# Two feed-forward half steps of a hybrid decoder layer: block products of 2x2 Strassen form in place of plain tiled products

## The chip, the cores and the metric

One core of a Trainium2 chip runs the whole step. The metric is device time in microseconds (us) of one launch. All arithmetic is float32: every large product is made from operands that are split in two float32r parts (a rounded "hi" and the rest "lo"), as hi·hi + hi·lo + lo·hi, so one product of a 128x128 weight tile and 260 tokens is three matmuls.

## The reference

One layer on 520 tokens (512 of a prompt and 8 single sample tokens), width 1024, feed-forward width 2816, followed by a final RMSNorm:

```python
x = x + 0.5 * swiglu(rmsnorm(x, n1), wg1, wu1, wd1)      # half step 1
x = x + token_mix(rmsnorm(x, nm), ...)                   # SSD scan heads and short conv, w_in, w_out
x = x + 0.5 * swiglu(rmsnorm(x, n2), wg2, wu2, wd2)      # half step 2
y = rmsnorm(x, nf)
def swiglu(x, wg, wu, wd): return (silu(x @ wg) * (x @ wu)) @ wd
```

## The kernel before

Activations lie with channels on the 128 partitions and the 520 tokens along the free axis, in two halves of 260 tokens; a matmul takes one weight tile (128x128) and one half.

A **weight unit** is up to eight such tiles of one output tile, 512 KB. `Core.fetch` and `split_w` (L89 to L92) load it on SP's queue into one of two `st` buffers, ScalarE rounds it to `hi` (L91), VectorE subtracts it to `lo` (L92); three pairs of buffers hold units that are ready, and the list `order` in `build` gives their sequence. `mm_unit` and `mm_k` (L115 to L124) walk the tiles of a unit with three products and two halves each, into a PSUM tile of two banks.

`ffn` (L270 and after) runs each half step. For each of 22 hidden tiles it makes the gate product and the up product (8 k-tiles each, 96 matmuls together), then on VectorE and ScalarE the factor of the norm, SiLU, the product of both and the two parts `hh`, `hl` (L283 to L291). For each of 8 output tiles it makes the way down over the 22 hidden tiles (132 matmuls), adds it to `x` (L299) and calls `after`, which prepares what the next stage needs: `Next` scales and splits x (L178, L179) and sums its squares on GpSimd (`square`, L143 to L147). Between the half steps stands `mixer` (L356 on). The last output tile of half step 2 is made by token halves, so that the final norm of the first half (`last`, L322 to L350) runs while the second is multiplied.

Instructions are put on the engines' queues by a scheduler that goes by its own timeline; each engine takes its queue in order. In the half steps GpSimd has nothing to do except the squares behind an output tile.

```python
 91  self.S.copy(hi, st)                                            # per weight unit, ScalarE
 92  self.V.tensor_tensor(lo, st, hi.bitcast(F32), op=ALU.subtract) # per weight unit, VectorE
```

Of the kernel before, what the change touches and what calls it, by code (L numbers as in the profile page):

```python
# [62 lines left out]

class Core:
    """The pieces that every phase uses: weight units, products, norm factors."""

    def __init__(self, nc, tc, ctx, a, order):
# [26 lines left out]
    def fetch(self):  # L94
        if self.at == len(self.order):
            return
        src, nk, *dt = self.order[self.at]
        self.at += 1
        st = self.wst.tile([P, KU, P], F32, tag="st", name="st")
        hi, lo = self.parts()  # L100
        if any(dt):  # both parts of the few dt weights in one stationary operand
            self.nc.sync.dma_start(st, src)
            s = slice(2 * NH, 3 * NH)
            self.S.copy(hi, st)
            self.V.tensor_tensor(hi[:, :, s], st[:, :, s], hi[:, :, s].bitcast(F32), op=ALU.subtract)
        else:
            self.split_w(src, st[:, :nk], hi[:, :nk], lo[:, :nk])
        self.ready.append((hi, lo, nk))

    def unit(self, ahead=1):  # L110
        while len(self.ready) < 1 + ahead and self.at < len(self.order):
            self.fetch()
        return self.ready.pop(0)

    def mm_k(self, ps, hi, lo, k, xh, xl, first, last, hs=(0, 1)):  # L115
        for n, (w, x) in enumerate(((hi, xh), (hi, xl), (lo, xh))):
            for h in hs:
# [18 lines left out]
    # RMSNorm: squares summed over the channel tiles here, over the partitions by a  # L136
    # product with ones; the factor of each token goes in behind the next product
# [3 lines left out]
    def square(self, acc, xt, first, eng):  # L141
        if first:
            eng.tensor_tensor(acc, xt, xt, op=ALU.mult)  # L143
        else:
            sq = self.nrm.tile([P, T], F32, tag="sq", name="sq", bufs=1)
            eng.tensor_tensor(sq, xt, xt, op=ALU.mult)  # L146
            eng.tensor_tensor(acc, acc, sq, op=ALU.add)  # L147

    def factor(self, accs, width):
        with self.tc.high_priority(2000):  # L150
            return self._factor(accs, width)

    def _factor(self, accs, width):
        r = self.nrm.tile([P, T], F32, tag="r", name="r")
        if len(accs) == 1:  # in two parts that sum to it
            ones = self.onesr
            hi = self.nrm.tile([P, T], F32R, tag="ah", name="ah", bufs=1)
            lo = self.nrm.tile([P, T], F32R, tag="al", name="al", bufs=1)
            self.S.copy(hi, accs[0])
            self.V.tensor_tensor(lo, accs[0], hi.bitcast(F32), op=ALU.subtract)  # L160
            accs = [hi, lo]
        else:
            ones = self.ones
        for h in range(2):
            hs = slice(h * H2, (h + 1) * H2)
            ps = self.bank()
            for i, acc in enumerate(accs):
                self.PE.matmul(ps[:, :H2], ones, acc[:, hs], start=i == 0, stop=i == len(accs) - 1)  # L168
            self.S.activation(r[:, hs], ps[:, :H2], AF.Sqrt, bias=self.eps, scale=1.0 / width)
            self.V.reciprocal(r[:, hs], r[:, hs])  # L170
        return r

    # what a product needs of x: x times the norm weight in two float32r parts
    def x_parts(self):
        return [self.xp.tile([P, KD, T], F32R, tag=n, name=n) for n in ("xh", "xl")]

    def split_x(self, xt, xh, xl, w):
        self.S.activation(xh, xt, AF.Copy, scale=w)  # L178
        self.V.scalar_tensor_tensor(xl, xt, w, xh.bitcast(F32), op0=ALU.mult, op1=ALU.subtract)  # L179
# [27 lines left out]

def build(nc, tc, ctx, a, o):
    order = []
    for f in range(1, KF):  # L210
        order += [(a["wg1"][f], KD), (a["wu1"][f], KD)]
    down = lambda w: [(w[d][:, k:min(k + KU, KF)], min(KU, KF - k)) for d in range(KD) for k in range(0, KF, KU)]
    order += down(a["wd1"])
    order += [(a["wi"][i], KD, i == 0) for i in range(a["wi"].shape[0])]
    for d in range(0, KD, 2):
        order += [(a["wo"][e][:, h:h + KD], KD) for h in (KD, 0) for e in (d, d + 1)]
    for f in range(KF):
        order += [(a["wg2"][f], KD), (a["wu2"][f], KD)]
    order += down(a["wd2"])
    c = Core(nc, tc, ctx, a, order)  # L220
# [4 lines left out]
    c.onesr = c.cst.tile([P, P], F32R, name="onesr")  # L225
    V.tensor_copy(c.onesr, c.ones)
# [4 lines left out]
    # the tensor engine's clock comes up while the first loads are under way  # L231
# [4 lines left out]
    # ---- input, with the first two weight units cut in pieces so that the products  # L236
    # can follow the loads
    x = [c.xp.tile([P, T], F32, tag=f"x{k}", name=f"x{k}") for k in range(KD)]
    xh, xl = c.x_parts()
    acc = [c.new_acc(), c.new_acc()]  # L240
    c0 = ExitStack()
    tp = c0.enter_context(tc.tile_pool(name="t0", bufs=2))
    u0 = [(a[w][0], tp.tile([P, KU, P], F32, tag="st", name="st")) + c.parts() for w in ("wg1", "wu1")]
    ps0 = [c.psum(), c.psum()]
    nc.sync.dma_start(c.pc, a["pc"])
    for k in range(KD):
        for h in range(2 if k == 0 else 1):
# [540 lines left out]
```

## Time and profile before

| | |
|---|---|
| median of 3 runs | 1196.25 us (1195.64 to 1198.01) |
| the profiled execution | span 1193.0 us from first to last instruction; its time outside the span is not given, the median is 3.25 us above the span |
| TensorE busy | 1163.1 us, 97% of the span, 9583 matmuls |
| VectorE, ScalarE, GpSimd busy | 632.9 (53%), 384.1 (32%), 254.0 us (21%) |
| granted TensorE clock, mean | 0.993 |
| half step 1, mixer, half step 2 | to about 395 us, to about 807 us, to the end |

A busy share is an average over stages with different limits, so a stage is read by itself. Spans of neighbouring instructions of one engine overlap by some tens of ns; where a price matters, the distance from one start to the next is taken.

### The profile page before, as it was taken

To read this page: it belongs to the slowest core of one execution; us is meant where nothing else is said; L and a number is where in the kernel's file an instruction comes from. 1 tells how busy PE (TensorE), PEld (TensorE's weight loads), DVE (VectorE), ACT (ScalarE), POOL (GpSimd) and SP (SyncE) were. 2 spreads that over 40 slices of the span, in tenths; PEclk is the share of its full clock that TensorE was granted. 3 is DMA by queue.
4 is the path that set the end of the run, shared out by engine and by line. 5 is a ranking of instruction groups with operands and counts; after the bars stand their busy time and mean duration, and the time that the engine had idled before them with its cause. 6 is when DMAs were issued, how large, how long until landed. Compare 5 with 4: busy or idle time off the path is not lost.

```text
span 1193.0 us, 22147 instructions
## 1 busy us (share of the span) xinstructions
PE 1163.1 (97%) x9583; PEld 1150.2 (96%) x9583; DVE 632.9 (53%) x810; ACT 384.1 (32%) x524; POOL 254.0 (21%) x318
## 2 busy tenths in 40 slices
PE   8999999999999999998899999999999999999996
PEld 7999999999999999987889999999999999999996
DVE  7544444443333678889987476445444444432224
ACT  5322222222222466344332343223222222222221
POOL 4000000000222377567643232320000000001112
PEclk8999999999999999999999999999999999999998
DMA  5322222222332432455533222222222222232322
GB/s 197 101 96 89 89 89 92 101 87 80 98 95 89 123 107 95 144 186 166 187 107 95 78 89 91 103 90 90 89 89 92 100 93 89 90 97 81 98 81 72
DMA packets 50361, 122.99 MB, mean 103 GB/s; under 512 B 9880, under 2 KB 19256, under 8 KB 50264
## 3 DMA queue, kind: packets, MB, share of 16 engines
q1 hardware_dynamic: 50264, 121.58, 31.4%
q8 instruction: 75, 1.23, 0.4%
q14 instruction: 22, 0.18, 0.0%
HBM read 114.43 MB, written 7.14 MB: 102 GB/s over the span
## 4 chain that ended last, share of the span: by engine, by line
PE 87%; POOL 4%; DVE 4%; issue 2%; DMA 2%; ACT 1%; SPq 0%; DVEq 0%; POOLq 0%; ACTq 0%
PE mmt L118 85%; POOL st L623 1%; POOL up L622 1%; DMA out_ss<-st 1%; DMA x<-in_xT 1%; DVE lo L92 1%; DMA st<-in_ssm 1%; DVE s L561 0%; POOL t L654 0%; POOL t L653 0%; DVE s L541 0%; PE auxt L168 0%; PE mmt L403 0%; POOL xd L616 0%; DVE up L625 0%
## 5 line engine op out<-in xcount | busy, mean ns | idle before, releaser
L118 PE MATMUL mmt<-xh,hi 128*128 128x260 f32 x2112 | 429.3, 284 | 1.7 <-ACT xh L178 1.7
L118 PE MATMUL mmt<-xh,lo 128*128 128x260 f32 x2112 | 426.8, 284 | 1.0 <-DVE lo L92 1.0
L118 PE MATMUL mmt<-xl,hi 128*128 128x260 f32 x2112 | 426.8, 284 | 0.8 <-DVE xl L179 0.7
L91 ACT CAST hi<-st 128x1024 fp32r<-128x1024 f32 (+2 forms) x202 | 202.6, 1005 | 644.0 <-issue 361.7
L92 DVE TENSOR_TENSOR lo<-st,hi 128x1024 fp32r<-128x1024 f32 (+2 forms) x202 | 245.2, 1215 | 177.9 <-ACT hi L91 176.7
L118 PEld LDWEIGHTS mmt<-xh,hi 128*128 128x128 f32 x2112 | 327.1, 189 | 2.8 <-ACT xh L178 1.9
L118 PEld LDWEIGHTS mmt<-xh,lo 128*128 128x128 f32 x2112 | 326.6, 189 | 1.8 <-DVE lo L92 1.6
L118 PEld LDWEIGHTS mmt<-xl,hi 128*128 128x128 f32 x2112 | 325.8, 189 | 1.6 <-DVE xl L179 1.5
L118 PE MATMUL mmt<-hh,hi 128*128 128x260 f32 x704 | 146.5, 285 | 0.0
L118 PE MATMUL mmt<-hh,lo 128*128 128x260 f32 x704 | 145.7, 283 | 0.0
L118 PE MATMUL mmt<-hl,hi 128*128 128x260 f32 x704 | 144.5, 281 | 0.0
L143 POOL TENSOR_TENSOR acc<-x 128x520 f32<-128x520 f32 x4 | 5.4, 1349 | 560.2 <-DVE x L299 538.0
L118 PEld LDWEIGHTS mmt<-hl,hi 128*128 128x128 f32 x704 | 110.6, 189 | 0.0
L118 PEld LDWEIGHTS mmt<-hh,hi 128*128 128x128 f32 x704 | 110.5, 189 | 0.1
L118 PEld LDWEIGHTS mmt<-hh,lo 128*128 128x128 f32 x704 | 109.3, 188 | 0.0
L287 DVE TENSOR_TENSOR h<-mmt,g 128x520 f32<-128x520 f32 x44 | 30.8, 700 | 124.3 <-PE mmt L118 124.2
L283 DVE TENSOR_TENSOR g<-mmt,r 128x520 f32<-128x520 f32 x44 | 30.8, 699 | 122.9 <-PE mmt L118 122.9
L146 POOL TENSOR_TENSOR sq<-x 128x520 f32<-128x520 f32 x22 | 35.4, 1609 | 196.6 <-DVE x L299 129.8
L147 POOL TENSOR_TENSOR acc<-acc,sq 128x520 f32<-128x520 f32 x28 | 43.8, 1563 | 2.2
L179 DVE SCALAR_TENSOR_TENSOR xl<-x,pc,xh 128x520 fp32r<-128x520 f32 (+1 forms) x25 | 32.8, 1323 | 4.8 <-ACT xh L178 4.8
L285 DVE TENSOR_TENSOR g<-g,r 128x520 f32<-128x520 f32 x44 | 30.4, 694 | 1.4 <-ACT g L284 1.4
L291 DVE TENSOR_TENSOR hl<-h,hh 128x520 fp32r<-128x520 f32 x44 | 30.5, 694 | 0.7 <-ACT hh L290 0.7
(193 smaller groups left out, 1015.2 us busy)
## 6 DMA issues: line engine op xcount, KB each, us to landing
st<-in_wi SPq DMA_DIRECT2D x45, 512.0 KB, 3.5
st<-in_wg SPq DMA_DIRECT2D x43, 512.0 KB, 3.5
st<-in_wu SPq DMA_DIRECT2D x43, 512.0 KB, 3.4
st<-in_wd SPq DMA_DIRECT2D x32, 512.0 KB, 3.4
st<-in_wo SPq DMA_DIRECT2D x16, 512.0 KB, 3.6
st<-in_wd SPq DMA_DIRECT2D x16, 384.0 KB, 3.1
st<-in_ssm SPq DMA_DIRECT2D x16, 256.0 KB, 2.8
s<-scr SPq DMA_DIRECT2D x8, 512.0 KB, 4.7
```

What stands on the lines that cost most here:

```text
L91: self.S.copy(hi, st)
L92: self.V.tensor_tensor(lo, st, hi.bitcast(F32), op=ALU.subtract)
L118: self.PE.matmul(ps[:, h, :H2], w[:, k, :], x[:, h * H2:(h + 1) * H2], start=first and n == 0, stop=last and n == 2)
L146: eng.tensor_tensor(sq, xt, xt, op=ALU.mult)
L147: eng.tensor_tensor(acc, acc, sq, op=ALU.add)
L179: self.V.scalar_tensor_tensor(xl, xt, w, xh.bitcast(F32), op0=ALU.mult, op1=ALU.subtract)
L283: V.tensor_tensor(halves(g), pg[:, :, :H2], halves(r), op=ALU.mult)
L285: V.tensor_tensor(g, g, r, op=ALU.mult)
L287: V.tensor_tensor(halves(hf), pu[:, :, :H2], halves(g), op=ALU.mult)
L291: V.tensor_tensor(b_, hf, a_.bitcast(F32), op=ALU.subtract)
L622: G.tensor_tensor(up, bb, xd.unsqueeze(2).broadcast_to([P, HB, NS]), op=ALU.mult)
L623: G.tensor_tensor(st, st, up, op=ALU.add)
```

## The change

Both operands of each feed-forward product are cut 2x2: the weights in output tiles m = 0, 1 and k-tiles in pairs, the activations in pairs of k-tiles and the two token halves. Seven block products of the Strassen-Winograd form replace eight.

- **Items.** A load (`load`) now brings a pair of output tiles and n pairs of k-tiles, four blocks a11, a12, a21, a22 of n·128 columns, 2048 columns (1 MB) for a gate or up item. `adds` makes four sums of blocks, S, in one buffer (pool `sp`, one buffer): s2 = a21 + a22, s0 = s2 - a11, s1 = a11 - a21, s3 = a12 - s0, all on GpSimd, except that s1 goes to VectorE where n is 3 or less. `split` then rounds and subtracts as before, but seven blocks instead of four: three units of two blocks (a11 and a12; s0 and s1; s2 and s3) and one of a22.
- **Groups.** `group` runs the seven block products of an item (`block`, 3n matmuls each) into three PSUM banks X, Z, Y of which X goes on accumulating while ScalarE copies its states out (`keep`) and VectorE adds bank and copy (`put`). There are 11 pairs of a gate and an up group (n = 4, 84 matmuls a group) in each half step.
- **Hidden tiles.** `variants` makes the seven operand blocks of a pair (three plain, four sums on VectorE) and their two parts. The product with the norm factor after SiLU (L407) goes to GpSimd.
- **Way down** in four chunks of hidden pairs (`CH`: 3, 3, 3, 2 pairs), of which three stand between a gate and an up group; in each chunk four groups add into `x`: VectorE adds the bank (L440), GpSimd adds ScalarE's copies (L442, three per group).
- **Around it.** `Blocks` scales x and makes its operand blocks at the start of a half step, `Plain` does what `Next` did for the mixer, squares behind a tile go to ScalarE. The final norm has both token halves of the last pair of tiles behind the last group. The mixer's products are as before; its buffers share memory with the new operands, and the scratch for S exists only inside a half step.

```diff
-    def split_w(self, src, st, hi, lo):
-        self.nc.sync.dma_start(st, src)
-        self.S.copy(hi, st)
-        self.V.tensor_tensor(lo, st, hi.bitcast(F32), op=ALU.subtract)
...
+    def adds(self):
+        for item in self.loaded:
+            kind, r, n, s = item[:4]
+            if kind != "S" or self.sp is None:
+                return
+            if s is None:
+                s = self.sp.tile([P, 4, 512], F32, tag="S", name="S")[:, :, :n * P]
+                item[3] = s
+                a11, a12, a21, a22 = (r[:, b] for b in range(4))
+                G = self.G
+                G.tensor_tensor(s[:, 2], a21, a22, op=ALU.add)
+                G.tensor_tensor(s[:, 0], s[:, 2], a11, op=ALU.subtract)
+                e = G if n > 3 else self.V
+                e.tensor_tensor(s[:, 1], a11, a21, op=ALU.subtract)
+                G.tensor_tensor(s[:, 3], a12, s[:, 0], op=ALU.subtract)
+                return
...
+            src = (r[:, :2], s[:, :2], s[:, 2:], r[:, 3])[step]
+            item.append(True)
+            hi, lo = self.parts(src, src.shape[1:])
+            self.both(src, hi, lo)
...
+    def block(self, ps, w, v, n, B, first, last):
+        hi, lo = (t.rearrange("p (k m) -> p k m", m=P) for t in w)
+        for k in range(n):
+            xh, xl = B(v, k)
+            for i, (a, b) in enumerate(((hi, xh), (hi, xl), (lo, xh))):
+                self.PE.matmul(ps[:, :H2], a[:, k, :], b, start=first and k + i == 0, stop=k == n - 1 and i == 2,
+                               skip_group_check=True)
...
+        w = self.take()
+        self.block(X, of2(w, 0), 0, n, B, True, True)
+        ev.p1(X)
+        self.block(Z, of2(w, 1), 1, n, B, True, True)
+        ev.c11(Z)
+        self.split()
+        w = self.take()
+        self.block(X, of2(w, 0), 5, n, B, False, True)
+        ev.u2(X)
+        self.block(Y, of2(w, 1), 4, n, B, True, True)
+        self.split()
+        w, w4 = self.take(), self.take()
+        self.block(X, of2(w, 0), 3, n, B, False, True)
+        ev.u4(X)
+        ev.c22(Y)
+        self.block(Y, w4, 6, n, B, False, True)
+        ev.c21(Y)
+        self.split()
+        self.block(X, of2(w, 1), 2, n, B, False, True)
+        ev.c12(X)
...
+    def c12(self, X):
+        c, g, r = self.c, self.dst, self.r
+        c.V.tensor_tensor(g[:, 0, T1], X[:, :H2], r[:, T1], op=ALU.mult)
+        c.V.tensor_tensor(g[:, 0, T0], g[:, 0, T0], r[:, T0], op=ALU.mult)
+        c.V.tensor_tensor(g[:, 1], g[:, 1], r, op=ALU.mult)
+        c.S.activation(g, g, AF.Silu)
+        c.G.tensor_tensor(g, g, r.unsqueeze(1).broadcast_to([P, 2, T]), op=ALU.mult)
```

The queues show it best in half step 1. First VectorE, in the gate and up stage. Before, one hidden tile has six rows (`g`, `h` its gate and up values, `st` a loaded weight unit, `hi` and `lo` its parts):

```order
L283 TENSOR_TENSOR g_1032<-mmt_922,r_293 128x520
L92 TENSOR_TENSOR lo_1046<-st_1044,hi_1045 128x1024
L285 TENSOR_TENSOR g_1032<-g_1032,r_293 128x520
L287 TENSOR_TENSOR h_1036<-mmt_923,g_1032 128x520
L92 TENSOR_TENSOR lo_1100<-st_1098,hi_1099 128x1024
L291 TENSOR_TENSOR hl6_1039<-h_1036,hh6_1038 128x520
```

Now the piece from one split of S to the same split of the next item (about half of what a pair of groups has; `pst` is a bank, `cp` ScalarE's copy, `raw` a loaded item, `S` its sums, `t4` the sums of a hidden pair):

```order
L149 TENSOR_TENSOR lo_2046<-S_1935,hi_2045 128x1024
L403 TENSOR_TENSOR g_1952<-pst_1953,r_233 128x260
L263 TENSOR_TENSOR hl_1941<-t4_1942,hh_1940 128x1040
L149 TENSOR_TENSOR lo_2067<-raw_1810,hi_2066 128x512
L382 TENSOR_TENSOR g_1952<-pst_1955,cp_1999 128x260
L405 TENSOR_TENSOR g_1952<-g_1952,r_233 128x520
L149 TENSOR_TENSOR lo_2109<-raw_1933,hi_2108 128x1024
L149 TENSOR_TENSOR lo_2139<-S_2072,hi_2138 128x1024
L382 TENSOR_TENSOR h_2077<-pst_2080,cp_2154 128x260
L420 TENSOR_TENSOR h_2077<-h_2077,g_1952 128x260
L149 TENSOR_TENSOR lo_2171<-S_2072,hi_2170 128x1024
```

The rows that read a bank are short; the rest take both operands from SBUF, and the split of S_2072 now waits on another engine's work.

That engine is GpSimd. Before, between the first norm's squares and the first output tile of the way down, it had no row at all; its neighbouring rows are these:

```order
L147 TENSOR_TENSOR acc_106<-acc_106,sq_226 128x520
L143 TENSOR_TENSOR acc_305<-x0_96 128x520
```

Now the same stretch of GpSimd that belongs to the VectorE rows above, a pair of groups:

```order
L132 TENSOR_TENSOR S_1935<-raw_1810 128x512
L135 TENSOR_TENSOR S_1935<-raw_1810 128x512
L133 TENSOR_TENSOR S_1935<-S_1935,raw_1810 128x512
L136 TENSOR_TENSOR S_1935<-raw_1810,S_1935 128x512
L132 TENSOR_TENSOR S_2072<-raw_1933 128x512
L135 TENSOR_TENSOR S_2072<-raw_1933 128x512
L133 TENSOR_TENSOR S_2072<-S_2072,raw_1933 128x512
L136 TENSOR_TENSOR S_2072<-raw_1933,S_2072 128x512
L407 TENSOR_TENSOR g_1952<-g_1952,r_233 128x1040
```

Eight sums of weight blocks and one long product per pair of groups stand where nothing stood.

## Rows read from the trace of the kernel before

**Rows 1.** Head and part 1 of the page: span, busy time of each engine.
```profile
span 1193.0 us, 22147 instructions
PE 1163.1 (97%) x9583; PEld 1150.2 (96%) x9583; DVE 632.9 (53%) x810; ACT 384.1 (32%) x524; POOL 254.0 (21%) x318
```
**Rows 2.** Stretches of half steps: PE, PEld, DVE, ACT, POOL busy, clock, DMA share, GB/s.
```profile
26.73:395.21 368.48, 368.48 (x3070) 368.48 (x3070) 152.79 (x170) 100.04 (x123) 21.46 (x13) 1.00 0.29 94
806.98:1172.00 365.02, 365.02 (x3042) 365.02 (x3041) 142.89 (x162) 98.39 (x122) 19.43 (x13) 1.00 0.28 89
```
**Rows 3.** Timeline of DVE at 396 us: start, length, instruction, shapes.
```profile
396.08 0.70 DVE L146 TENSOR_TENSOR sq<-x 128x520 f32<-128x520 f32 x1
396.69 1.22 DVE L92 TENSOR_TENSOR lo<-st,hi 128x1024 fp32r<-128x1024 f32 x1
397.83 0.17 DVE L446 TENSOR_SCALAR nega<-nega 128x16 f32<-128x16 f32 x1
```
**Rows 4.** Timeline at 777 us, DVE and POOL.
```profile
777.11 2.09 DVE L92 TENSOR_TENSOR lo<-st,hi 128x1024 fp32r<-128x1024 f32 x1 [0.19 <-ACT hi L91]
779.12 1.80 DVE L179 SCALAR_TENSOR_TENSOR xl<-x,pc,xh 128x520 fp32r<-128x520 f32 x1
777.07 1.05 POOL L146 TENSOR_TENSOR sq<-x 128x520 f32<-128x520 f32 x1 [1.89 <-DVE x L716]
778.20 2.17 POOL L147 TENSOR_TENSOR acc<-acc,sq 128x520 f32<-128x520 f32 x1
```
**Rows 5.** Timeline at 1101 us, DVE and POOL.
```profile
1101.59 0.96 DVE L92 TENSOR_TENSOR lo<-st,hi 128x768 fp32r<-128x768 f32 x1
1101.80 1.66 POOL L146 TENSOR_TENSOR sq<-x 128x520 f32<-128x520 f32 x1 [12.80 <-DVE x L299]
1103.54 1.31 POOL L147 TENSOR_TENSOR acc<-acc,sq 128x520 f32<-128x520 f32 x1
```
**Rows 6.** Timeline at 512 us, DVE and POOL; mmt and auxt are PSUM.
```profile
512.63 0.69 DVE L642 TENSOR_TENSOR u<-mmt,t 128x520 f32<-128x520 f32 x1
513.24 0.74 DVE L557 TENSOR_TENSOR xd<-auxt,dt 128x256 f32<-128x256 f32 x2
512.77 1.27 POOL L623 TENSOR_TENSOR st<-st,up 128x512 f32<-128x512 f32 x1
```
**Rows 7.** Tile view of ce: ns min/median/max, first and last start.
```profile
L538 POOL TENSOR_TENSOR ce<-ce,xs x4: 2395/2400/2495, 500.5 to 639.0; 128x1024 f32<-128x1024 f32 x4
```
**Rows 8.** ACT by line and shape, 26 to 390 us: busy us, mean ns.
```profile
L91 ACT CAST hi<-st 128x1024 fp32r<-128x1024 f32 x56 | 58.8, 1049 | 226.4 <-issue 159.0 <-PE mmt L118 66.3 <-DMA st<-in_wg 1.1
L284 ACT ACTIVATE g<-g 128x520 f32<-128x520 f32 x22 | 13.9, 635 | 0.0
```
**Rows 9.** Part 6 of the page: one weight unit's load, median us to landing.
```profile
st<-in_wg SPq DMA_DIRECT2D x43, 512.0 KB, 3.5
```
**Rows 10.** Critical chain of the first 40 us: start, us, what.
```profile
14.68 3.27 DVE xl L179 x2
24.98 1.75 PE auxt L168 x8
26.73 13.33 PE mmt L118 x111
```
**Rows 11.** Critical chain at 795 to 812 us, mixer to half step 2.
```profile
794.91 11.00 PE mmt L118 x92
805.91 0.24 PE auxt L168 x2
806.14 0.60 PE mmt L118 x5
```
**Rows 12.** Critical chain from 1160 us to the end.
```profile
1176.02 5.40 PE mmt L118 x45
1181.44 0.44 DVE x L309
1187.74 1.01 DVEq L774
```
**Rows 13.** Stretches of the mixer around a pause of PE, columns as in rows 2.
```profile
560.40:563.80 3.40, 0.02 (x2) 0.03 (x2) 3.33 (x6) 0.45 (x2) 2.00 (x2) 1.00 0.64 224
563.80:567.20 3.40, 3.40 (x24) 2.08 (x24) 3.40 (x7) 2.56 (x6) 3.40 (x5) 0.62 0.48 166
```

More of the change, by code (lines that the diff above doesn't have):

```diff
@@ L110, in unit, with load @@
-    def unit(self, ahead=1):
-        while len(self.ready) < 1 + ahead and self.at < len(self.order):
-            self.fetch()
+        self.items, self.loaded, self.steps, self.ready = items, [], [], []
+        self.next_load = 0
+        self.sp = None
+    def load(self, pieces=1):
+        if self.next_load == len(self.items):
+            return
+        kind, src, n = self.items[self.next_load]
+        self.next_load += 1
+        t = self.raw.tile([P, 4 * 512], F32, tag="raw", name="raw")
+        if kind == "S":
+            r = t[:, :4 * n * P].rearrange("p (b m) -> p b m", b=4)
+            for i in range(pieces):
+                s = slice(i * 4 // pieces, (i + 1) * 4 // pieces)
+                self.nc.sync.dma_start(r[:, s], src[:, s])
+        else:
+            r = t[:, :n * P]
+            self.nc.sync.dma_start(r, src)
+        self.loaded.append([kind, r, n, None])
@@ L113, in unit, with prime, take, mm_k @@
+    def prime(self):
+        while len(self.ready) < 4 and self.loaded:
+            self.split()
+    def take(self):
+        if not self.ready:
+            self.split()
         return self.ready.pop(0)
-    def mm_k(self, ps, hi, lo, k, xh, xl, first, last, hs=(0, 1)):
+    def mm_k(self, ps, hi, lo, k, xh, xl, first, last):
         for n, (w, x) in enumerate(((hi, xh), (hi, xl), (lo, xh))):
-            for h in hs:
+            for h in (0, 1):
                 self.PE.matmul(ps[:, h, :H2], w[:, k, :], x[:, h * H2:(h + 1) * H2],
@@ L149, in factor @@
     def factor(self, accs, width):
         with self.tc.high_priority(2000):
[L151 to L171, printed above, removed]
@@ L174, in x_parts @@
[L174 to L179, printed above, removed]
+            r = self.nrm.tile([P, T], F32, tag="r", name="r")
+            for h in range(2):
+                hs = slice(h * H2, (h + 1) * H2)
+                ps = self.bank()
+                for i, acc in enumerate(accs):
+                    self.PE.matmul(ps[:, :H2], self.ones, acc[:, hs], start=i == 0, stop=i == len(accs) - 1)
+                self.S.activation(r[:, hs], ps[:, :H2], AF.Sqrt, bias=self.eps, scale=1.0 / width)
+                self.V.reciprocal(r[:, hs], r[:, hs])
@@ new lines, in ffn_items @@
+def ffn_items(a, n):
+    gate, up, down = a[f"wg{n}"], a[f"wu{n}"], [a[f"wd{n}{i}"] for i in range(len(CH))]
+    way = lambda i: [("S", down[i][e], len(CH[i])) for e in range(NQ)]
+    items = []
+    for p in range(NP):
+        items.append(("S", gate[p], NQ))
+        if p in BEHIND:
+            items += way(BEHIND[p])
+        items.append(("S", up[p], NQ))
+    return items + way(len(CH) - 1)
+def build(nc, tc, ctx, a, o):
+    items = ffn_items(a, 1)
+    items += [("dt" if i == 0 else "P", a["wi"][i], KD) for i in range(a["wi"].shape[0])]
+    for d in range(0, KD, 2):
+        items += [("P", a["wo"][e][:, h:h + KD], KD) for h in (KD, 0) for e in (d, d + 1)]
+    items += ffn_items(a, 2)
+    c = Core(nc, tc, ctx, a, items)
@@ L234, in build @@
         PE.matmul(ps[:, :P], c.ones, c.ones, start=True, stop=True)
[L238 to L239 removed]
+    x = [c.xp.tile([P, 2, T], F32, tag=f"x{e}", name=f"x{e}") for e in range(NQ)]
+    nx1 = Blocks(c, x, "n1")
+    nx1.begin()
+    nc.sync.dma_start(c.pc, a["pc"])
     acc = [c.new_acc(), c.new_acc()]
[L241 to L243 removed]
@@ L312, in build, with ffn, down, Bh @@
-    nxt = Next(c, x, "nm")
-    ffn(xh, xl, r, ps0, nxt, False)
-    nx2 = Next(c, x, "n2")
+    for e in range(NQ):
+        for m in range(2):
+            nc.sync.dma_start(x[e][:, m], a["xT"][2 * e + m])
+        if e == 0:
+            c.load(pieces=2)
+    c.load()
+    def ffn(nx, start, after, halves_last=None):
+        with ExitStack() as c2:
+            pool = lambda name, bufs, **k: c2.enter_context(tc.tile_pool(name=name, bufs=bufs, **k))
+            c.sp = pool("sp", 1)
+            fp = pool("fp", 1)
+            hp = pool("hp", 3)
+            pp = pool("pp", 6, space=bass.MemoryType.PSUM)
+            bank = lambda: pp.tile([P, 512], F32, tag="ps", name="pst")
+            if start:
+                for e in range(NQ):
+                    nx.operands(e)
+                    if e == 0:
+                        c.adds()
+                        c.split()
+                    for m in range(2):
+                        if e < 2:
+                            c.square(acc[0], x[e][:, m], e + m == 0)
+                        elif e + m == 2:
+                            S.activation(acc[1], x[e][:, m], AF.Square)
+                        else:
+                            c.square(acc[1], x[e][:, m], False, True)
+                c.prime()
+                r = c.factor(acc, D)
+            else:
+                c.prime()
+                r = nx.factor()
+            hv = {}
+            B = lambda v, k: nx[v, k]
+            def down(i):
+                ps = CH[i]
+                def Bh(v, k):
+                    hh, hl = hv[ps[k]]
+                    return hh[:, v], hl[:, v]
+                final = i == len(CH) - 1
+                for e in range(NQ):
+                    half = (lambda h, e=e: halves_last(e, h)) if final and halves_last and e == NQ - 1 else None
+                    c.group(len(ps), Bh, bank, Down(c, fp, x[e], half))
+                    if final:
+                        if e == 0:
+                            c.table(AF.Sqrt, x[0][:, 0, :1])
+                        if not half:
+                            after(e)
+            for p in range(NP):
+                g = fp.tile([P, 2, T], F32, tag="g", name="g")
+                c.group(NQ, B, bank, Gate(c, fp, g, r))
+                if p in BEHIND:
+                    down(BEHIND[p])
+                h = c.tv.tile([P, 2, T], F32, tag="xw", name="h")
+                c.group(NQ, B, bank, Up(c, fp, h, g))
+                hh, hl = (hp.tile([P, 7, H2], F32R, tag=n, name=n) for n in ("hh", "hl"))
+                c.variants(h, hh[:, :3], hl[:, :3], hh[:, 3:], hl[:, 3:])
+                hv[p] = hh, hl
+            down(len(CH) - 1)
+            c.sp = None
@@ L351, in last @@
                 nc.sync.dma_start(o["yT"][:, e0:e1, ts], y[:, e0:e1, ts])
-    ffn(nx2.xh, nx2.xl, nx2.factor(), None, last, True)
+    ffn(nx2, False, last, last_half)
 def mixer(c, o, x, nxt, nx2):
```

399 lines of the change are left out of this document (243 added, 156 removed).

## The prediction

> **What bounds the kernel now.** I read the page's busy times first: TensorE is busy 1163 of 1193 us [rows 1]. The two stretches that make up most of the half steps confirm it stage by stage: PE is busy without a gap and the clock is whole. 368.48 us for 3070 matmuls is **0.120 us per matmul** [rows 2]. VectorE is busy there 153 of 368 us, ScalarE 100, GpSimd 21. So a half step lasts as long as its matmuls, and the other engines have slack. Whether they keep it is the question, because the change takes work from TensorE and gives work to the others. The third view is the timeline of VectorE beside GpSimd, in the few places where both run today.
>
> **What TensorE saves.** A half step has 22 x 96 + 8 x 132 = 3168 matmuls of 260 columns. With seven blocks for eight it has 2772; over both half steps 792 go, 6336 become 5544. At 0.120 us that is **760 us before and 665 us after, 95 us saved**, if TensorE stays the bound. The price holds for the new order too: every matmul has its own weight load before and after, and the 45 matmuls into one bank near the end take 5.40 us, again 0.120 [rows 12]. (The Trainium skill, page "TensorE: Matmul & The Clock Gate", section "Wait — 56ns, not 53.3ns?", gives N/2.4 GHz plus 2.5 ns from start to start; for 260 columns that would be an estimate of 111 ns and 88 us saved. The rows say 120 ns, so the measurement decides.)
>
> **What the other engines get, and a resource that the busy shares hide.** At 777 us GpSimd starts a square 0.04 us ahead of VectorE's `lo`. GpSimd takes its 1.05 us; `lo` takes 2.09 us instead of 1.22, so it stood still until GpSimd was done. Then it turns: GpSimd's sum, 1.31 us when alone, takes 2.17 [rows 3 to 5]. At 1101 us VectorE came first and the square of 1.05 us took 1.66 [rows 4, 5]. So a VectorE instruction with both inputs in SBUF and a GpSimd instruction on SBUF **exclude each other**. A VectorE instruction that reads PSUM does not pay: at 512.63 us it keeps its 0.69 us beside a GpSimd sum of 1.27 [rows 6]. In the half steps of today this costs nothing, as GpSimd has next to no work there. After the change it has work in every group, and I add both engines' SBUF work as if they were one engine.
>
> Prices for VectorE, start to start: 0.61 us for 520 elements and 1.14 for 1024 [rows 3]; on that line 0.33 for 256 and 0.34 for 260, 0.47 for 384, 0.60 for 512, 0.87 for 768, 1.16 for 1040. From PSUM, 0.74 us for two of 256, so some 0.33 each [rows 6]. For GpSimd: 1.27 for 512 and 1.31 for 520 with two inputs [rows 5, 6], by proportion 0.95 for 384 and 0.65 for 256 or 260, and 2.45 for 1040 from 2.40 for 1024 [rows 7].
>
> *A pair of gate and up groups.* VectorE, both inputs in SBUF: weight parts 6 x 1.14 + 2 x 0.60 = 8.04; products with r and g, 2 x (0.34 + 0.61) = 1.90; operand blocks of the hidden pair 2 x 0.61 + 3 x 0.34 + 1.16 = 3.40; together 13.3. GpSimd: 8 x 1.27 + 2.45 = 12.6. Sum **26.0 us**, against 168 x 0.120 = 20.2 us of TensorE (before: two hidden tiles, 23.0). VectorE's eight PSUM rows (2.6 us) are not in it, since they run beside GpSimd. (The Trainium skill, page "SBUF — State Buffer", section "Who interferes with whom", speaks against the change: it says the engines share a port pair that one instruction holds whole, and that an instruction with at most one SBUF input stays clear of it. Had PSUM rows to queue as well, the sum here would be 28.6; the one case in the trace goes with the page, and its rule leaves the sum at 26.0.)
>
> *A way-down group of three pairs* (24 of them): VectorE 3 x 0.87 + 0.47 + 0.47 for s1 = 3.55, GpSimd 3 x 0.95 + 3 x 0.65 = 4.80; sum 8.35, TensorE 63 x 0.120 = 7.6. *Of two pairs* (8): 2.46 + 3.87 = 6.3, TensorE 5.0; in half step 1 two `xl` (0.61 each, priced as 520 elements) and two sums of squares (1.31 each) come on top, 10.2; in half step 2 the two sums alone, in three of four groups, 9.0.
>
> Sum: 22 x 26.0 + 24 x 8.35 + 4 x 10.2 + 3 x 9.0 + 6.3 = **846 us**, 181 above TensorE's new 665 and 86 above the old 760. That is the floor, with the shared way never idle.
>
> It will be idle sometimes. S has one buffer. From the split that empties it, the queue shows three sums on GpSimd with VectorE's SBUF rows between them (3.87 us with gaps, plus 1.16 + 0.60 + 0.61 + 1.14 = 3.5), then ScalarE's rounding of s0, s1 (1.05 us [rows 8]), VectorE's subtraction (1.14), the next rounding and subtraction: about 11.8 us. The other half of the pair has 1.4 us more of VectorE's work and L407 (2.45) between, so 15.7. **27.5 us per pair**; with waits on bank copies I take 28.0, and the same 7% on the rest: 616 + 216 + 80 = **912 us, 152 more than before**. Queued behind the split of S on VectorE are the sums that free the banks, so TensorE then waits for both. That is what is late next.
>
> ScalarE gets about 13 us per pair: 7.4 for rounding weights, 2.6 for six bank copies, 1.2 for SiLU, 2.1 for operands, scaled from the rows there are [rows 8]; hidden under 26. Loads: the same bytes in 1 MB pieces; 512 KB lands in 3.5 us [rows 9], so 1 MB within 7, and two buffers give it a group of 10 us or more: hidden by the groups; without that cover 7 us each.
>
> **Around the half steps.** *Start:* today the first 96 matmuls follow the loads and the factor is in at 26.7 us; of that 96 x 0.120 = 11.5 is work, 15 is not; two `xl` in a row take 3.27 instead of 1.2 beside GpSimd's squares [rows 10]. Now four sets of operand blocks (4 x 3.40) and 12 us of squares and sums exclude each other, 26 us from about 7 us on, when the first x is there: 33 without a full group, 18 more, less some 3 for the groups' work done in gaps, +15 (5 to 25). *Into half step 2:* today the change of stage costs 0.5 us [rows 11]. Now the scratch for S is free only when the last w_out product is done, then four sums beside the last operand blocks: 5.1 + 3.4, +9 (3 to 12). *Into the mixer:* +2 (0 to 5). *End:* the norm of the first token half had 5.40 us of matmuls over it [rows 12]; now one block of 6 matmuls, 0.7 us: +4 (0 to 6). The mixer's matmuls are unchanged and its squares leave GpSimd; I take 0 (-8 to +8). Together **+30**.
>
> 1193.0 + 152 + 30 = 1375 us of span; the median lies 3.25 above the span, so **1378 us**.
>
> **Rivals.**
> - *TensorE keeps the pace* and the change is faster. It needs the exclusion to be weaker than read: the sum per pair must fall from 26.0 below 20.2, that is, GpSimd's 12.6 us must run for some 6 us beside VectorE's SBUF rows. For it: VectorE alone needs 13.3 + 2.6 = 16 us and GpSimd 12.6, both under 20.2. Against it: both directions of the exclusion in rows 4. Time: 1196 - 95 + 30 = 1131. Chance 0.06.
> - *The single S buffer and the bank copies wait in a chain*, each engine idle in turn, 31 us per pair and 10 and 85 for the rest. For it: queues in order, and splits that wait for three engines. Time: 22 x 31 + 24 x 10 + 85 = 1007, so 1196 + 247 + 30 = 1473. Chance 0.12.
> - *The clock falls.* After a stretch in which PE was busy 0.02 of 3.40 us, the granted clock was 0.62 in the next, half of it at the lower level [rows 13]. With pauses of 8 us in 28 the clock could go to half often. The Trainium skill, page "TensorE: Matmul & The Clock Gate", section "What's actually happening", says throttled is the default and activity lifts it. In the mixer matmuls with shorter pauses than that one kept the whole clock. If half of the 5544 matmuls took twice 0.120, 333 us come to TensorE's 665; 998 is then above 912, and the time 1196 + 238 + 30 = 1464 or, with waits between, some 1500. Chance 0.06.
>
> **Numbers.** The forecast has 0.76. The range goes from 1275 (the floor of 846 with a few us of transitions gives 1196 + 86 + 10 = 1292, less 2% for prices of shapes that were scaled) to 1480 (the chain, 1473). Below it lie the first rival and a little more, above it most of the clock's case. A measurement tells about 0.2% from no change. Faster 0.06 is the first rival, same 0.01, slower 0.93.
>
> **What would show it.** Right: in the gate and up stages VectorE and GpSimd together show hardly an idle moment, GpSimd's 512-wide sums last well over 1.27 us in the mean and `lo` of 1024 well over 1.22; PE is busy about 70%, with its pauses ended by VectorE or ScalarE; a pair takes about 28 us. Wrong: `lo` stays at 1.22 with sums running beside it and a pair takes 20 to 21 us (first rival); or GpSimd and VectorE both wait for long and pairs take over 30; or the granted clock is far below 1 in the half steps.

## The result, and the profile after

The changed kernel takes **1343.4 us** (1343.0 to 1344.4), the kernel before beside it 1196.8: ratio 1.1224, 95% interval 1.1208 to 1.124. The profiled execution has a span of 1341.5 us, 148.5 more than before [rows 1].

The head and part 1 of the page of the changed kernel:

```profile
span 1341.5 us, 21910 instructions
PE 1153.5 (86%) x8795; PEld 1108.3 (83%) x8795; DVE 1119.1 (83%) x1357; ACT 604.7 (45%) x952; POOL 796.9 (59%) x692
```

788 matmul records are gone (792 by the forecast's count), yet TensorE's busy time fell by 10 us only; part of the rest ran at the lower clock (0.948 granted in the mean, 0.993 before). VectorE went from 633 to 1119 us, GpSimd from 254 to 797. The page's chain of waits, by engine, says who sets the end now; before it was almost all PE:

```profile
DVE 43%; PE 30%; POOL 11%; issue 8%; ACT 6%; DMA 2%; DVEq 0%; SPq 0%; ACTq 0%; POOLq 0%
```

Stretches of the changed kernel (columns as in rows 2): the start, two pairs of a gate and an up group, one pair with four way-down groups, and the last gate group to the end.

```profile
26.00:44.00 18.00, 12.45 (x63) 11.20 (x64) 15.29 (x14) 8.65 (x14) 12.94 (x7) 0.81 0.16 59
...
189.96:240.36 50.40, 42.00 (x316) 40.95 (x315) 47.25 (x53) 21.21 (x34) 30.03 (x17) 0.93 0.22 74
240.36:303.36 63.00, 55.65 (x445) 53.68 (x445) 56.90 (x64) 30.80 (x50) 47.27 (x34) 1.00 0.27 92
...
1274.70:1341.50 66.80, 38.96 (x234) 33.91 (x232) 44.69 (x66) 26.48 (x52) 36.01 (x34) 0.79 0.21 56
```

The windows are cut at the start of L403, which each gate group has once. A pair takes 50.40 / 2 = **25.2 us** (mean of the 12 such intervals from 102 us on: 25.3), where its 168 matmuls need 20.2 at 0.120. A way-down group of three pairs takes (63.00 - 25.2) / 4 = **9.45** (mean of 24: 9.6) against 7.6. VectorE is busy 94% of the two pairs, against 41% in [rows 2]. From the last gate group to the end PE is busy 39 of 66.8 us.

Why VectorE is so busy is in the durations, by line and shape, of VectorE and GpSimd:

```profile
L149 DVE TENSOR_TENSOR lo<-raw,hi 128x1024 fp32r<-128x1024 f32 x104 | 171.1, 1645 | 26.3 <-ACT hi L148 25.4
L442 POOL TENSOR_TENSOR x<-x,cp 128x260 f32<-128x260 f32 x96 | 103.7, 1087 | 71.6 <-DVE x L440 52.8 <-ACT hh L262 9.0 <-ACT cp L434 8.4
L135 POOL TENSOR_TENSOR S<-raw 128x512 f32<-128x512 f32 x44 | 83.3, 1894 | 0.0
L407 POOL TENSOR_TENSOR g<-g,r 128x1040 f32<-128x1040 f32 x22 | 65.0, 2954 | 20.9 <-ACT g L406 20.5
L132 POOL TENSOR_TENSOR S<-raw 128x512 f32<-128x512 f32 x44 | 59.4, 1349 | 133.7 <-DVE lo L149 130.3 <-PE mmt L197 2.1 <-DMA raw<-in_wg 1.3
```

The subtraction of 1024 elements takes 1645 ns in the mean, where 1.22 us is its time alone [rows 3]; the sum L135 of 512 takes 1894 where [rows 6] had 1.27 us for that size, L407 of 1040 takes 2954 where 1024 took 2400 [rows 7]. L442 adds the bank copies of the way down, L132 waits for the split that empties S. The timeline of the changed kernel from 190 us on shows the turn-taking, VectorE first:

```profile
190.30 2.22 DVE L263 TENSOR_TENSOR hl<-t,hh 128x1040 fp32r<-128x1040 f32 x1
192.44 1.78 DVE L149 TENSOR_TENSOR lo<-raw,hi 128x512 fp32r<-128x512 f32 x1
194.14 0.42 DVE L382 TENSOR_TENSOR g<-pst,cp 128x260 f32<-128x260 f32 x1
194.48 1.94 DVE L149 TENSOR_TENSOR lo<-raw,hi 128x1024 fp32r<-128x1024 f32 x1
...
212.51 1.22 DVE L149 TENSOR_TENSOR lo<-S,hi 128x1024 fp32r<-128x1024 f32 x1
```

GpSimd in the same stretch, and then TensorE:

```profile
190.12 1.29 POOL L132 TENSOR_TENSOR S<-raw 128x512 f32<-128x512 f32 x1 [5.43 <-DVE lo L149]
191.38 2.29 POOL L135 TENSOR_TENSOR S<-raw 128x512 f32<-128x512 f32 x1
193.63 1.71 POOL L133 TENSOR_TENSOR S<-S,raw 128x512 f32<-128x512 f32 x1
```

```profile
193.66 0.28 PE L213 MATMUL pst<-vth,lo 128*128 128x260 f32 x1
196.48 0.39 PE L213 MATMUL pst<-vbh,lo 128*128 128x260 f32 x1 [2.54 <-DVE lo L149]
```

L132 starts first and takes its 1.29; `hl` of 1040 elements, started 0.18 later, takes 2.22. L135 then waits for `hl`, the next `lo` (512 elements, 1.78) waits for L135, and so on down the line. The row from PSUM at 194.14 keeps its 0.42. At 212.51, with GpSimd idle, `lo` of 1024 is back at 1.22. TensorE's first matmul after 193.66 that needs the `lo` of 194.48 starts at 196.48: the idle 2.54 us are the price of the row's place in that queue. Over the whole run TensorE waits longest for this kind of row (us in total, times, longest):

```profile
PE pst L213 <- DVE lo L149: 102.7, 66, 4.4
```

The chain of waits at the stage changes and at the end:

```profile
470.07 5.32 PE mmt L665 x28
...
883.18 0.71 DVE x L986
...
1322.53 2.04 PE auxt L585 x8
1324.59 0.48 ACT rf L587
1325.10 2.60 DVE rf L596 x2
1327.70 3.79 DVE y L599 x4
```

For comparison, the last residual sum of the mixer in VectorE's timeline of the kernel before, which answers to 883.18 here:

```profile
799.25 0.70 DVE L716 TENSOR_TENSOR x<-mmt,x 128x520 f32<-128x520 f32 x1 [2.21 <-PE mmt L118]
```

**Where the 148.5 us lie.** By the trace the last way-down product of half step 1 ends at 469.4 (before 395.2), the mixer's last at 883.2 (before 799.3), the last of half step 2 at about 1321 (before 1181.4), and 20.5 us follow it (before 11.6). (The table ahead lets the mixer of the kernel before end at about 807 us. That is where the norm factor of half step 2 is done; its first gate products start at 799.05, so the mixer ends there.) Inside the half steps, 22 x 25.3 + 24 x 9.63 + 77 for the last chunks = 865 us, **105 more** than 760, about 55 of it in the first. So the start costs 74.2 - 55 = 19, the mixer 413.8 - 404.1 = 10, the way into half step 2 437.8 - 382.1 - 50 = 6, the end 8.9. Together 149.

### The profile page after: what moved, and what is told of

Read it like the earlier page. It is cut to its first block, busy times and chain, and to the rows that moved or that the text cites. A ratio compares the mean times of both kernels' runs of the same rounds, so it can differ in the third digit from the quotient of the medians.

```text
span 1341.5 us, 21910 instructions
## 1 busy us (share of the span) xinstructions
PE 1153.5 (86%) x8795; PEld 1108.3 (83%) x8795; DVE 1119.1 (83%) x1357; ACT 604.7 (45%) x952; POOL 796.9 (59%) x692
## 4 chain that ended last, share of the span: by engine, by line
DVE 43%; PE 30%; POOL 11%; issue 8%; ACT 6%; DMA 2%; DVEq 0%; SPq 0%; ACTq 0%; POOLq 0%
DVE lo L149 21%; PE mmt L197 17%; PE pst L213 10%; ACT hi L148 4%; DVE hl L263 3%; POOL x L442 2%; DVE S L135 2%; DVE t L254 2%; DVE h L421 2%; DVE g L382 1%; POOL S L133 1%; POOL up L886 1%; POOL S L132 1%; DVE h L382 1%; POOL st L887 1%
## 5 line engine op out<-in xcount | busy, mean ns | idle before, releaser
L149 DVE TENSOR_TENSOR lo<-raw,hi 128x1024 fp32r<-128x1024 f32 (+2 forms) x212 | 321.5, 1522 | 26.3 <-ACT hi L148 25.4
L149 DVE TENSOR_TENSOR lo<-S,hi 128x1024 fp32r<-128x1024 f32 (+2 forms) x152 | 207.6, 1366 | 60.1 <-ACT hi L148 59.3
L148 ACT CAST hi<-raw 128x1024 fp32r<-128x1024 f32 (+2 forms) x212 | 174.1, 832 | 144.3 <-PE mmt L197 82.8
L213 PE MATMUL pst<-vbh,lo 128*128 128x260 f32 x528 | 159.0, 315 | 70.0 <-DVE lo L149 69.9
L132 POOL TENSOR_TENSOR S<-raw 128x512 f32<-128x512 f32 (+2 forms) x76 | 96.0, 1263 | 188.2 <-DVE lo L149 184.7
L213 PE MATMUL pst<-vth,hi 128*128 128x260 f32 x704 | 199.9, 288 | 8.2 <-ACT hi L148 6.9
L213 PE MATMUL pst<-hh,lo 128*128 128x260 f32 x616 | 174.7, 302 | 31.5 <-DVE lo L149 31.3
L213 PE MATMUL pst<-vtl,hi 128*128 128x260 f32 x704 | 198.9, 285 | 2.3 <-DVE vtl L263 2.3
L213 PE MATMUL pst<-vth,lo 128*128 128x260 f32 x704 | 192.0, 285 | 1.5 <-DVE lo L149 1.4
L213 PE MATMUL pst<-hh,hi 128*128 128x260 f32 x616 | 178.9, 301 | 15.6 <-ACT hi L148 5.6
L213 PE MATMUL pst<-hl,hi 128*128 128x260 f32 x616 | 177.8, 295 | 4.5 <-DVE hl L260 2.5
L442 POOL TENSOR_TENSOR x<-x,cp 128x260 f32<-128x260 f32 x96 | 103.7, 1087 | 71.6 <-DVE x L440 52.8
```

The lines of the kernel that those rows point to most:

```text
L132: G.tensor_tensor(s[:, 2], a21, a22, op=ALU.add)
L148: self.S.copy(hi, src)
L149: self.V.tensor_tensor(lo, src, hi.bitcast(F32), op=ALU.subtract)
L213: self.PE.matmul(ps[:, :H2], a[:, k, :], b, start=first and k + i == 0, stop=k == n - 1 and i == 2, skip_group_check=True)
L442: c.G.tensor_tensor(x, x, t, op=ALU.add)
```

## Experiments

The theory under test: VectorE's rows with two SBUF inputs and GpSimd's rows exclude each other, and the sum of both sets the pair. Rivals: a chain of waits through the one S buffer and the bank copies, and TensorE with its clock.

**1. `ports`: the exclusion by itself.** The kernel computes nothing of the step; it runs rows of both engines, each alone and then beside each other.

```diff
+    dve(1024, 16, "aloneV")
+    gp(512, 16, "aloneG")
+    dve(1024, 16, "bothV")
+    gp(512, 16, "bothG")
+    dve(260, 40, "bankV", ps)
+    gp(512, 16, "bankG")
+    act(1024, 16, "actS")
+    gp(512, 16, "actG")
```

> This kernel computes nothing of the step; it runs stretches of sixteen VectorE subtractions (1024 wide, both inputs in SBUF) and sixteen GpSimd sums (512 wide), each alone and then together, then forty VectorE rows with one input in PSUM (260 wide) beside sixteen GpSimd sums, and ScalarE copies beside GpSimd sums. If the engines exclude each other, alone is 16 x 1.14 = 18 us and 16 x 1.25 = 20 us, together 38 us; with PSUM input or with ScalarE the pair ends with GpSimd at 20 us. If they only share bandwidth or do not meet, together ends at 20 to 25 us.

Timeline of VectorE and GpSimd (4 or 16 rows in one line):

```profile
9.92 18.25 DVE L226 TENSOR_TENSOR aloneV<-x,y 128x1024 f32<-128x1024 f32 x16
53.95 34.33 DVE L226 TENSOR_TENSOR bothV<-x,y 128x1024 f32<-128x1024 f32 x16
...
31.32 19.54 POOL L232 TENSOR_TENSOR aloneG<-x,y 128x512 f32<-128x512 f32 x16 [28.73 <-DVE x L248]
54.06 35.37 POOL L232 TENSOR_TENSOR bothG<-x,y 128x512 f32<-128x512 f32 x16 [3.21 <-DVE x L248]
93.10 19.64 POOL L232 TENSOR_TENSOR bankG<-x,y 128x512 f32<-128x512 f32 x16 [3.67 <-DVE x L248]
139.76 9.36 POOL L232 TENSOR_TENSOR longG<-x,y 128x1040 f32<-128x1040 f32 x4 [3.67 <-DVE x L248]
```

The rows with a bank as input, in the view by line:

```profile
L226 DVE TENSOR_TENSOR bankV<-ps,y 128x260 f32<-128x260 f32 x40 | 13.5, 413 | 0.0
L238 ACT COPY actS<-x 128x1024 f32<-128x1024 f32 x16 | 15.2, 1041 | 107.7 <-DVE x L248 107.7
```

Alone 18.25 and 19.54 us, together 35.4, some 2 us below the 38 of full exclusion: 2.21 us for one row of each, where 1.14 + 1.22 = 2.36 would be full exclusion. So for rows of these two shapes some 0.15 us per GpSimd row are hidden, and no more. GpSimd keeps its time beside 40 VectorE rows that read PSUM (19.64 us) and those keep theirs, 0.34 each. (The Trainium skill, page "SBUF — State Buffer", section "Who interferes with whom", says that a VectorE instruction with at most one SBUF input, outside the modes that use two ports, does not contend with GpSimd, and that ScalarE never waits on anyone; both rows agree.) With these prices, and the 0.15 taken for every GpSimd row, a pair is by estimate 13.4 of VectorE + 8 x 1.22 + 2.34 of GpSimd (1040 wide, alone: `longG`) - 9 x 0.15 = **24.1 us**, against the 26.0 that I had summed.

**2. `nosum`: the sums alone taken away.** The S sums are left out: the splits read the loaded blocks in their place, all else is kept.

```diff
-                G.tensor_tensor(s[:, 2], a21, a22, op=ALU.add)
...
+                item[3] = s = r
...
-            src = (r[:, :2], s[:, :2], s[:, 2:], r[:, 3])[step]
+            src = (r[:, :2], r[:, :2], r[:, 2:], r[:, 3])[step]
```

> Leaves out the four sums of weight blocks per item (the blocks that were loaded are split in their place), on both engines; matmuls, splits and evacuations stay. Exclusion: VectorE keeps 15.9 us per gate and up pair, GpSimd only 2.45, so TensorE with 20.2 us becomes the bound again: pairs of 20.2 to 21.5 us instead of 25.2, way-down groups of 7.6 to 8 instead of 9.5, the time 1195 to 1225 us. If VectorE's own load were the bound (it reads 93% busy), the pair would stay at 24 to 25 us and the time at 1310 to 1340.

1168.8 us in one run, below the 1195 to 1225 that I had expected. Windows, two pairs and then a pair with four way-down groups:

```profile
160.65:200.48 39.83, 39.83 (x334) 39.83 (x333) 33.16 (x53) 24.18 (x37) 5.67 (x3) 1.00 0.26 93
200.48:251.75 51.27, 51.17 (x427) 50.97 (x426) 38.79 (x59) 28.74 (x47) 12.83 (x12) 1.00 0.32 114
```

A pair takes 19.9 us with PE never idle: TensorE's pace, at a whole clock. So the sums, with what they do to their neighbours, cost 1343 - 1169 = 175 us; the group order, the bank copies and the splits do not slow TensorE in these stretches. Even so, only 27 of the 95 us saved on paper would be left of the time before: the rest goes at the start, in the last chunks, in the mixer and at the end. From its first matmul to its last a last chunk takes 38.5 us in half step 1 (346.3 to 384.8) and 34.3 in half step 2 (1114.0 to 1148.3); some 36 matmuls of the up group stand among its 168, and all together need 24.5 at 0.120.

**3. `s2buf`: the chain through the S buffer.** Two S buffers; to make room, four bank copies in place of six.

```diff
-        t = self.pool.tile([P, H2], F32, tag="cp", name="cp", bufs=6)
+        t = self.pool.tile([P, H2], F32, tag="cp", name="cp", bufs=4)
...
-            c.sp = pool("sp", 1)
+            c.sp = pool("sp", 2)
```

> Two buffers for the sums S instead of one (and four bank copies instead of six to make room). If the chain through the single buffer set the pace, GpSimd's 40% of idle time would be used, pairs would come down to 22 or 23 us and the time to about 1290 us. Exclusion: the same work in another order, pairs stay at 25 us, time 1335 to 1350 us.

1343.4 us (1337.5 to 1345.8), ratio to before 1.1232 (1.1211 to 1.1254): the same as the change. The windows of two pairs, and of a pair with four groups, and the first sum in the view by line:

```profile
191.94:239.83 47.89, 43.02 (x323) 41.79 (x322) 45.41 (x55) 23.64 (x37) 27.01 (x16) 0.93 0.23 78
239.83:304.58 64.75, 55.42 (x439) 53.15 (x438) 53.64 (x62) 28.45 (x47) 50.93 (x36) 1.00 0.26 90
```

```profile
L132 POOL TENSOR_TENSOR S<-raw 128x512 f32<-128x512 f32 x44 | 66.0, 1500 | 89.9 <-DMA raw<-in_wg 61.3 <-DVE t L257 16.5 <-DVE lo L149 5.5
```

GpSimd's wait for the split that empties S (130 us before L132) is gone; now it waits for the load. A pair falls to 23.9 us, close to the 24.1 estimated in the first experiment, and no further. So waits through S cost some 1.2 us a pair, not 5. What is won there is lost in the way-down groups, 10.2 us (9.45 before); whether the two bank copies fewer or the order of the sums did that, this run does not tell apart.

**4. `sumsV`: the sums on the engine that is already the busiest.**

```diff
-                G = self.G
+                G = self.V
```

> All four sums of an item go to VectorE, with the product after SiLU and the sums into x left on GpSimd. Exclusion: a sum of 512 costs 0.60 on VectorE instead of 1.25 on GpSimd, so a pair needs 13.3 + 8 x 0.60 + 2.45 = 20.6 of excluded work and VectorE in all 20.7 plus the wait for GpSimd's 2.45: 23.2 us instead of 25.2; way-down groups 7.6 to 8.3 instead of 9.5; time 1250 to 1280 us. If VectorE's load alone were the bound, 4.8 us more per pair: 30 us, time about 1450 us.

1267.1 us (1262.2 to 1268.5), ratio 1.0581 (1.0556 to 1.0605): 76 us better than the change, on an engine that gets eight more rows a pair. Windows as above, and one row each of VectorE's and GpSimd's timelines:

```profile
175.29:218.13 42.84, 40.27 (x327) 39.30 (x326) 42.64 (x66) 22.03 (x33) 5.54 (x2) 1.00 0.24 87
218.13:277.05 58.92, 54.96 (x433) 53.71 (x433) 56.28 (x86) 31.40 (x49) 17.08 (x13) 0.97 0.28 99
```

```profile
204.81 2.81 DVE L133 TENSOR_TENSOR S<-S,raw 128x512 f32<-128x512 f32 x1
...
204.64 2.44 POOL L407 TENSOR_TENSOR g<-g,r 128x1040 f32<-128x1040 f32 x1 [18.17 <-ACT g L406]
```

A sum of 512 takes 0.61 us from start to start on VectorE and 1.22 on GpSimd, and on either it shuts the other out: moved, it costs half. A pair takes 21.4 us, less than the 23.2 expected, and VectorE is busy 42.64 of 42.84. The 2.81 are a sum that met GpSimd's L407, the row that still excludes. The groups stay at 9.4, against the 7.6 to 8.3 expected; L442 is still GpSimd's there.

**5. `allV`: the other two GpSimd rows as well.**

```diff
-        c.G.tensor_tensor(g, g, r.unsqueeze(1).broadcast_to([P, 2, T]), op=ALU.mult)
+        c.V.tensor_tensor(g, g, r.unsqueeze(1).broadcast_to([P, 2, T]), op=ALU.mult)
...
-            c.G.tensor_tensor(x, x, t, op=ALU.add)
+            c.V.tensor_tensor(x, x, t, op=ALU.add)
```

> Besides the sums S, the product after SiLU and the sums into x go to VectorE too; GpSimd has no work in the half steps but the squares. VectorE per pair: 13.4 + 4.9 + 1.2 + 2.6 from PSUM = 22.1 us, above TensorE's 20.1; way-down groups 7.3 us of VectorE against 7.6 of TensorE. Exclusion: pairs of 22 to 22.5 us, groups of 7.7 to 8.2, time 1215 to 1245 us. If the latency of the queues (S made late, split late) decides instead of the sum of the work, groups stay at the 9.6 us that they have with the sums alone moved, and the time stays above 1250.

1234.2 us (1231.6 to 1237.3), ratio 1.0323 (1.0299 to 1.0347). Windows, and the split of the sums by line:

```profile
169.24:211.27 42.03, 39.81 (x326) 39.13 (x326) 41.02 (x69) 22.34 (x34) 0.00 (x0) 1.00 0.25 89
211.27:267.35 56.08, 53.55 (x434) 52.40 (x434) 54.56 (x99) 29.93 (x48) 0.00 (x0) 1.00 0.29 104
```

```profile
L149 DVE TENSOR_TENSOR lo<-S,hi 128x1024 fp32r<-128x1024 f32 x88 | 106.6, 1221 | 11.2 <-ACT hi L148 11.2
```

With GpSimd empty, `lo` is at 1221 ns. Pairs take 21.0, below the 22 to 22.5 expected, groups 8.8, above the 7.7 to 8.2, and VectorE alone is the bound (98% busy). All of the change's arithmetic on one engine beats its division over two by 109 us, and still loses to the kernel before by 38.

**6. `downonly`: seven products only where VectorE has room.** The gate and up products stay plain as in the kernel before; the way down keeps its four chunks; all sums on VectorE.

```diff
-                c.group(NQ, B, bank, Gate(c, fp, g, r))
-                if p in BEHIND:
-                    down(BEHIND[p])
...
+                for m in range(2):
...
+                    plain(gm, r)
+                    S.activation(gm, gm, AF.Silu)
+                    V.tensor_tensor(gm, gm, r, op=ALU.mult)
+                    plain(h[:, m], gm)
+                    if m == 0 and p in BEHIND:
+                        down(BEHIND[p])
```

> Seven products for eight on the way down only, its weight sums and its sums into x on VectorE; gate and up as in the kernel before, plain, and so are the operands of x and the start. 924 matmuls instead of 1056 per half step save 264 x 0.120 = 31.6 us. VectorE has 10.4 + 3.4 = 14 us of work in 23 us of gate and up, and 7.3 in 7.6 us of a way-down group. Exclusion (no GpSimd work beside it, so TensorE stays the bound): 1196 - 32, plus 7 at the end, where the last norm is no longer covered, plus 0 to 10 for groups that VectorE holds up: 1168 to 1185 us, faster than both. If the seven-product groups wait in their own chains, 9.6 us a group and 24 x 2 = 48 us more: 1215 to 1230.

1211.6 us (1210.3 to 1213.5), ratio 1.0137 (1.0117 to 1.0156): a miss, some 30 us above what I had expected. The windows say where: 100 us of plain products with a chunk among them, and the last chunk of either half step.

```profile
100.00:200.00 100.00, 100.00 (x835) 100.00 (x834) 68.74 (x123) 38.48 (x55) 0.00 (x0) 1.00 0.29 96
...
366.00:403.00 37.00, 26.67 (x168) 23.78 (x168) 33.18 (x62) 22.59 (x44) 10.42 (x6) 0.82 0.21 72
...
1160.00:1191.00 31.00, 24.09 (x160) 21.62 (x160) 27.50 (x56) 20.30 (x41) 10.04 (x6) 0.91 0.10 34
```

Chunks with plain products around them run at TensorE's pace, VectorE at 69%. The short last chunk stands alone: 168 matmuls that need 20 us take 37 in half step 1 and 32 in half step 2 (whose window leaves out the first microsecond), with VectorE the busiest engine. I had priced the groups by their mean and not by their neighbours. Nor was GpSimd out of the way, as the expectation had it: its six rows for the squares of the next norm (10.4 and 10.0 us) fall into just these windows. In half step 1 `vtl`, the rest part of x for the mixer, takes 1.80 us beside one of them and 0.75 at 383.8 us, with GpSimd idle:

```profile
387.07 1.80 DVE L321 SCALAR_TENSOR_TENSOR vtl<-x,pc,vth 128x520 fp32r<-128x520 f32 x1
...
386.24 2.08 POOL L279 TENSOR_TENSOR acc<-acc,sq 128x520 f32<-128x520 f32 x1 [3.94 <-ACT sq L276]
```

How much of the loss is theirs, no run takes apart.

**7. `plainlast`: the last chunk plain.** Seven products in the first three chunks only; the last two pairs multiply plainly, in half step 2 the last two output tiles by token halves; the first product's banks are kept, so that the next need not wait.

```diff
-CH = [(0, 1, 2), (3, 4, 5), (6, 7, 8), (9, 10)]
+CH = [(0, 1, 2), (3, 4, 5), (6, 7, 8)]
+PL = (9, 10)
...
-            down(len(CH) - 1)
+            for e in range(NQ):
+                hi, lo, nk = c.take()
+                b = [[bank(), bank()] for m in range(2)]
...
+                    for k, (kh, kl) in enumerate(hp2):
+                        for m in range(2):
+                            for n, (w, xx) in enumerate(((hi, kh), (hi, kl), (lo, kh))):
```

> Seven products only for the first three chunks of the way down, as in the run with the way down alone; the last chunk (two pairs, four k-tiles) multiplies plainly, its last two output tiles by token halves in half step 2 so that the first half's norm lies beside the second half's products, and the first product's sums keep PSUM banks of their own, so that the next product needn't wait for them. Everything of the step is computed. 24 groups of 63 matmuls stand where 24 x 72 stood: 216 fewer x 0.120 us = 26 us, so 1170 where TensorE keeps its pace throughout. Theory (what the version with the way down alone lost lay in its short last chunk, 17 + 12 us over 20 us at pace, at the start, some 6 us, and in the end, some 12 us, while groups of three pairs ran at TensorE's pace): 1172 to 1188 us, ratio 0.98 to 0.993, gate and up products and chunk groups at 0.119 to 0.121 us a matmul. Rival (the sums and splits of the chunks cost time wherever they stand, 24 groups of at least 1 us each): 1195 us or more.

**1178.7 us** (1177.0 to 1180.3), ratio 0.9858 (0.9836 to 0.9879): 1.4% faster than the kernel before, and in the middle of the first theory's range. Its page, two of its windows, and the chain at its end:

```profile
PE 1140.9 (97%) x9371; PEld 1125.4 (96%) x9371; DVE 801.8 (68%) x1298; ACT 472.3 (40%) x686; POOL 220.5 (19%) x301
```

```profile
126.00:226.00 100.00, 100.00 (x835) 100.00 (x834) 68.16 (x120) 38.98 (x56) 0.00 (x0) 1.00 0.29 97
226.00:326.00 100.00, 100.00 (x835) 100.00 (x834) 68.62 (x121) 38.78 (x57) 0.00 (x0) 1.00 0.29 97
```

```profile
1139.94 19.88 PE pst L618 x166
```

TensorE has no gap in these 200 us, and its last 166 matmuls run in one piece at 0.120. The span is 16.2 us shorter than before: 14.5 in half step 1 and 12.8 in half step 2, where 108 matmuls less in each make 13, minus 5.7 that the mixer and 5.4 that the end cost more (17.0 us behind the last product, 11.6 before).

## Why the prediction was right, and where its sizes were off

- **TensorE's saving** of 95 us, if it stays the bound: the price held (`nosum`: 168 matmuls of a pair in 19.9 us); the condition did not, as forecast.
- **The exclusion** was the cause: taking GpSimd's rows away (`nosum`, `sumsV`, `allV`) removed 175, 76 and 109 us, though in the last two VectorE got the work. Rows from PSUM stay clear, as read from one pair of rows.
- **The pair, the mis-sized term:** 26.0 as floor and 28.0 taken; the floor comes to 24.1 by the prices of `ports` (`s2buf` reaches 23.9), and 25.3 were measured. Of the floor's 1.9 us, 1.35 are the 0.15 that each of nine GpSimd rows hides, the rest GpSimd's prices: 1.22 for 512 elements and 2.34 for 1040 where I took 1.27 and 2.45. The waits came to 1.2, not 2.0. Over 22 pairs 59 us too much.
- **Way-down groups:** 8.35 with 7% = 9.0 taken, 9.6 measured, 15 us too little over 24. The last chunks: 80 taken, 77 measured.
- **Around the half steps:** start 15 taken, 19 measured, and little of it is the weight sums: without them (`nosum`) the first gate group reaches its L403 at 48.9 us instead of 52.6, at a clock of 0.64 from 26 to 44 us where the change had 0.81. Into half step 2, 9 taken, 6 measured. The end, 4 taken, 9 measured: the chain after the last product now holds the square sums, both token halves' factors and products (1322.5 to 1331), where before the first half's lay under 5.40 us of matmuls [rows 12].
- **The mixer, taken at 0 with 2 on the way in, cost 10.** Set beside the same rows of the kernel before, its rows come later and later: the lag grows by some 4 us up to the first product that is read out of its bank, by 6 among the short convolutions (2 to 5 in the other versions) and by 1 after. Its buffers, its weight queue and the place of its splits all changed at once. No run takes these apart, so the cause stays open.
- **The sign "PE is busy about 70%"** did not come: 42.0 of 50.40 us are 83%. The others did: VectorE busy 94%, stretched rows on both engines, and pauses of PE that VectorE's `lo` ends.
- **Sum:** 182 forecast against 148.5, all inside the range; the half steps were 47 too high and what lies around them 14 too low, so a part of the nearness is luck. The range's lower end was worked out wrongly: 1292 less 2% is 1266, not 1275.
- **The rivals.** That TensorE keeps the pace needed a pair's sum below 20.2: it is 24.1. The chain through S: the wait is in the rows (GpSimd idle 130 us before L132), but a second buffer gives the pair 1.2 us and the time nothing. The reading under the clock's rival was off: 0.62 in the second stretch of [rows 13] is three quarters of it at the lower level (0.92 in its first microsecond, then 0.50), not half; the rival's price did not use it. In the changed kernel the clock fell after pauses (0.81 in 26 to 44 us, 0.93 in the two pairs, 0.948 in the mean), but there VectorE was the later one, and `allV` at a clock of 1.00 over its two pairs still takes 21.0 a pair.

## What to carry to other kernels

Add up VectorE's two-input SBUF rows and GpSimd's rows as one resource before dividing work between them: where that sum sets the pace, as in these pairs, a sum that GpSimd takes off VectorE at twice the duration makes the pair slower, not faster. An algorithm that saves matmuls pays only in the stretches where the engines that prepare its operands have slack left, so try it stage by stage, and price the last stage by itself, where nothing else stands beside it.

## What the runs showed of the hardware

The exclusion is not quite whole: a VectorE row of 1024 and a GpSimd row of 512 in turn take 2.21 us where the two alone take 2.36. And the loser of a turn is not one engine: GpSimd's 16 sums went from 19.5 to 35.4 us and VectorE's 16 subtractions from 18.3 to 34.3, so each showed near-double durations while the work of both together hardly gained.
